# First two modulation chunks on TensorE in four column strips, in place of row sums on VectorE and GpSimd

## Chip, cores and metric

One core of a Trainium2 chip runs the kernel. The metric is the device time of one execution in microseconds; the time given for the kernel before is the median of three runs. TensorE multiplies matrices, VectorE, ScalarE and GpSimd work on tiles of up to 128 partitions, and transfers from device memory are issued by SyncE (its queue is SP's) and GpSimd.

## What is computed

One layer of a diffusion backbone in float32, for 512 latent tokens and 256 context tokens of 1024 channels. Only its beginning matters here: an RMS norm whose result is modulated by shift and scale, two of six chunks of `silu(c) @ w_mod + b_mod`, for the latent by `c` and for the context by `c_ctx`.

```python
def _modulate(x, g, shift, scale):
    return _rmsnorm(x, g) * (1.0 + scale) + shift

m_x = (silu(c) @ w_mod + b_mod).reshape(B, 6, 1, 1024)
m_c = (silu(c_ctx) @ w_mod + b_mod).reshape(6, 1024)
hc = _modulate(ctx, g_norm1, m_c[0], m_c[1])
pc = hc @ w_in[:, :1280]
hx = _modulate(x, g_norm1, m_x[:, 0], m_x[:, 1])
px = hx @ w_in
```

What follows takes `px` and `pc`: a recurrent branch (RG-LRU, five heads), a gMLP branch with spatial gating, their merge under two sigmoid gates, an output projection, a second norm, a channel mixer with a 3x3 convolution, and a final norm. Chunks 2 to 5 of the modulation are used there.

## The kernel before

Tokens lie along the free dimension and channels over the partitions ("channel-major"): 1024 channels are eight channel tiles of 128. Nearly every large product runs as three float32r matmuls: weights and activations are each split into two float32r parts that sum to the float32 value (`wh`, `wl`; `hxh`, `hxl`), and the low-by-low product is left out. The class `Weights` (line 55) loads weight blocks in the order in which TensorE takes them, through SP's queue into two buffers, casts the high part on ScalarE (line 95) and subtracts it on VectorE or GpSimd (line 97). `W.load` asks for a block's transfer, `W.prepare` splits up to a block, `W.take` hands over the next one.

The first stage (lines 218 to 355) is the one that the change touches.

- Loads, all on SP's queue: `crow` (both `c` vectors as 16 rows), `xc` (all 768 tokens, eight transfers of 384 KB), the packed parameters `sm`, then `w_mod` by channel tile (`wm`, 1 MB each, four buffers) alternating with the first weight blocks.
- Conditioning: `sig` is silu of `crow`; 16 matmuls against slices of the identity spread both vectors over all partitions (line 253), and copies bring them to `cbx` and `cbc`.
- Norm: squares on ScalarE (line 262), their sums over channel tiles on VectorE for the latent (line 263) and on GpSimd for the context (line 264), sums over partitions by a matmul with ones (line 274), root and reciprocal, and `spread_rows` (line 205) to bring the factor of every token to all partitions; the result is `rb`.
- Modulation of channel tile k: `mod_rows` takes the dot products of the rows of `wm` with `cbx` and `cbc`, four per tile (shift and scale, latent and context). The table `MOD_ON` says for each whether VectorE does it in one operation (line 303) or GpSimd multiplies (line 297) and ScalarE sums (line 298). `mod_cols` adds the bias and multiplies by `g1`. `mod_h` multiplies x by `rb` and scale (line 330, VectorE), casts the high part with the shift added (line 331, ScalarE) and makes the low part (line 332, VectorE).
- `products(k)` adds channel tile k's part to nine outputs that stay in PSUM (line 314): two tiles of `rx` for the latent, the same two for the context (`rxc`), two of `rg` and three of the merge's first gate `gr` (`NFIRST`). These are 27 matmuls for a tile, 21 of 512 columns and 6 (the context's) of 256; the other `gr` tiles are computed later, before the gates of heads that `GR_AT` names.

Two channel tiles are modulated ahead of the first products (`LEAD`), then one for each step. The build's scheduler decides the order of each engine's instructions: by the order in the program, except that one which it holds to be ready goes ahead of one that is not; `after` fixes an order by hand. On the chip each engine keeps the order it was given.

Chunks 2 to 5 of the modulation come later, row by row of `w_mod` from GpSimd's queue (lines 554 to 569), against `cbx` and `sc`. The change leaves them as they are; line 613, the spatial gating's float32 matmul, is also unchanged.

Of the kernel before, what the change touches and what calls it, by code (L numbers as in the profile page):

```python
# [42 lines left out]
# Columns of the packed per-channel parameters.  # L43
# [66 lines left out]
def hybrid_block(ctx: ExitStack, tc: tile.TileContext, a: dict, out: bass.AP):  # L110
# [107 lines left out]
    with pool("pro", side="right") as pro:  # L218
        crow = pro.tile([2 * KD, P], F32, name="crow")
        nc.sync.dma_start(crow, a["c_row"])  # L220
        xc = pro.tile([P, KD, TT], F32, name="xc")
        for k in range(KD):
            nc.sync.dma_start(xc[:, k, :], a["xc"][k])
        nc.sync.dma_start(sm, a["smalls"])
        wms = {}

        def load_mod(k):
            wms[k] = pro.tile([P, 2, D], F32, tag="wm", name=f"wm{k}", bufs=4)
            nc.sync.dma_start(wms[k], a["w_mod01"][k].rearrange("p (s c) -> p s c", s=2))
# [12 lines left out]
        # silu(c), silu(c_ctx) in every partition.  # L242
        sig = pro.tile([2 * KD, P], F32, name="sig")
        nc.scalar.activation(sig, crow, AF.Sigmoid)
        nc.vector.tensor_tensor(sig, sig, crow, op=ALU.mult)
        cb = (cbx, pro.tile([P, D], F32, name="cbc"))
        cbp = {}
        for n in range(2):
            for hf in range(2):
                pb = cbp[n, hf] = mm_tile(f"cb{n}{hf}")  # L250
                for q in range(4):
                    kk = KD * n + 4 * hf + q
                    nc.tensor.matmul(pb[:, q * P : (q + 1) * P], ident[: 2 * KD, kk : kk + 1].to_broadcast([2 * KD, P]), sig,
                                     start=True, stop=True)
        psc = mm_tile("psc")
        nc.tensor.transpose(psc[:, : 2 * KD], sig, ident[: 2 * KD, : 2 * KD])
        nc.vector.tensor_copy(sc, psc[:, :KD])
        sqs = pro.tile([P, TT], F32, name="sqs")
        nc.scalar.activation(sqs, xc[:, 0, :], AF.Square)
        for k in range(1, KD):  # L260
            sq = pro.tile([P, TT], F32, tag="sq", name=f"sq{k}", bufs=4)
            squared = nc.scalar.activation(sq, xc[:, k, :], AF.Square)
            nc.vector.tensor_tensor(sqs[:, TC:], sqs[:, TC:], sq[:, TC:], op=ALU.add)
            nc.gpsimd.tensor_tensor(sqs[:, :TC], sqs[:, :TC], sq[:, :TC], op=ALU.add)
        for (n, hf), pb in cbp.items():
            if (n, hf) != (1, 1):
                nc.vector.tensor_copy(cb[n][:, hf * T : (hf + 1) * T], pb)
        after(nc.scalar.copy(cb[1][:, T:], cbp[1, 1]), squared)
        # The latent's tokens first.
        rb = pro.tile([P, TT], F32, name="rb")  # L270
        for t0, n, slot in ((2, 4, 0), (0, 2, 1)):
            pss = aux_tile(f"pss{t0}", slot)
            for t in range(n):
                mm = nc.tensor.matmul(pss[:, t : t + 1], sqs[:, (t0 + t) * P : (t0 + t + 1) * P], ones[:, 0:1],
                                      start=True, stop=True)
                if t0 == 0 and t == 0:
                    after(mm, summed)
                summed = mm
            r = rstd_of(pro, pss[:, :n], f"n1{t0}", n)
            prb = aux_tile(f"rb{t0}", slot)[:, : n * P]  # L280
            spread_rows(prb, r, n)
            copied = nc.scalar.copy(rb[:, t0 * P : (t0 + n) * P], prb)
# [3 lines left out]
        gr_ps = {j: mm_tile(f"gr{j}") if j < 2 else aux_tile(f"gr{j}", 1) for j in range(NFIRST)}  # L286
# [4 lines left out]
        def mod_rows(k, n, ms):  # L291
            """Shift (2 n) and scale (2 n + 1) sums of channel tile k for x (n = 0) or ctx (n = 1)."""
            for s in range(2):
                o = ms[:, 2 * n + s : 2 * n + s + 1]
                if MOD_ON[k][2 * n + s] == "G":
                    junk = pro.tile([P, D], F32, tag="pjunk", name=f"pj{k}{s}{n}", bufs=3)
                    nc.gpsimd.tensor_tensor(junk, wms[k][:, s, :], cb[n], op=ALU.mult)  # L297
                    act = nc.scalar.activation(junk, junk, AF.Copy, accum_out=o)  # L298
                    if k == 0:
                        after(act, copied)  # L300
                else:
                    junk = pro.tile([P, D], F32, tag="junk", name=f"vj{k}{s}{n}", bufs=1)
                    nc.vector.scalar_tensor_tensor(junk, wms[k][:, s, :], 1.0, cb[n],  # L303
                                                   op0=ALU.mult, op1=ALU.mult, accum_out=o)

        def products(k, wh, wl):
            xs = ((hxh[:, k, :], hxl[:, k, :]), (hch[:, k, :], hcl[:, k, :]))
            outs = [(rx_ps[j][0], j, *xs[0]) for j in range(2)] + [(rx_ps[j][1], j, *xs[1]) for j in range(2)]
            outs += [(rg_ps[j], 2 + j, *xs[0]) for j in range(2)] + [(gr_ps[j], 4 + j, *xs[0]) for j in range(NFIRST)]
            for i, (o, j, xh, xl) in enumerate(outs):  # L310
                c = slice(j * P, (j + 1) * P)
                for n, (w, x) in enumerate(((wh, xh), (wh, xl), (wl, xh))):
                    first, last = k == 0 and n == 0, k == KD - 1 and n == 2
                    mm = nc.tensor.matmul(o, w[:, c], x, start=first and i != 3, stop=last and i != 2)
                    if (first or last) and i in (2, 3):
                        if i == 3:
# [5 lines left out]
        def mod_cols(k, ms, n0, n1):  # L322
            m = ms[:, 2 * n0 : 2 * n1].rearrange("p (n s) -> p n s", s=2)
# [608 lines left out]
```

## Time and profile before

| | |
|---|---|
| median of 3 runs | 1013.49 us (1010.37 to 1014.34) |
| profiled execution, span from first to last instruction | 1015.3 us |
| TensorE, matmuls busy | 956.4 us (94%) |
| VectorE busy | 710.9 us (70%) |
| ScalarE busy | 489.3 us (48%) |
| GpSimd busy | 150.1 us (15%) |

Of the profiled execution the profile gives the span and no other time, so the two stand side by side in the table. Busy time is an average over the whole kernel; what an engine is worth in one stage is read from the stretch in which the stage lies. "PE" is TensorE's matmuls, "PEld" its weight loads, "DVE" VectorE, "ACT" ScalarE, "POOL" GpSimd. Matmuls are pipelined, so that their listed durations overlap: what one costs in a row of them is the distance between starts.

### The profile page before, as it was taken

What the parts mean: (1) busy time and instruction counts of PE and PEld (TensorE: products, weight loads), DVE (VectorE), ACT (ScalarE), POOL (GpSimd) and SP (SyncE); (2) the same over time, 40 slices, a digit from 0 to 9 for tenths busy, and PEclk for the clock granted to TensorE, in tenths of its full rate; (3) what the DMA queues carried; (4) which work ended last, traced back from release to release, by engine and by line L of the source; (5) the groups of instructions that cost most, each with busy time, mean ns of one, the idle gap of its engine ahead of it and who ended that gap; (6) DMA issues with size and microseconds to landing.
All of it is one profiled execution on the core that took longest, in us unless ns stands there. A gap on an engine that the chain in (4) does not pass through costs nothing.

```text
span 1015.3 us, 11483 instructions
## 1 busy us (share of the span) xinstructions
PE 956.4 (94%) x4547; PEld 794.2 (78%) x4547; DVE 710.9 (70%) x894; ACT 489.3 (48%) x675; POOL 150.1 (15%) x113
## 2 busy tenths in 40 slices
PE   4568999999999999989999998999999999999997
PEld 4357888888888878878888888988767888887686
DVE  6999849696766776567653356598778437888864
ACT  5445697888799682114323334344333213333333
POOL 7661000000000011110100112212220003222020
PEclk9979999999999999999999999999999999999999
DMA  9422221222222247653632621122212332221232
GB/s 361 150 97 83 83 83 43 83 76 70 87 101 83 83 167 240 257 207 106 213 138 83 212 108 75 45 81 83 83 63 84 124 138 90 83 84 63 66 122 83
DMA packets 22325, 116.29 MB, mean 115 GB/s; under 512 B 2544, under 2 KB 2688, under 8 KB 13312
## 3 DMA queue, kind: packets, MB, share of 16 engines
q1 hardware_dynamic: 16448, 94.59, 25.8%
q0 software_dynamic: 5824, 20.97, 6.0%
q8 instruction: 35, 0.57, 0.2%
q14 instruction: 18, 0.15, 0.0%
HBM read 113.46 MB, written 2.10 MB: 114 GB/s over the span
## 4 chain that ended last, share of the span: by engine, by line
PE 59%; DVE 21%; ACT 9%; issue 6%; DMA 3%; POOL 1%; SPq 0%; ACTq 0%; POOLq 0%; DVEq 0%
DVE acc L798 8%; PE d L142 4%; PE d L141 4%; PE d L143 4%; PE up L143 4%; PE up L141 4%; PE up L142 4%; DVE wl L97 3%; DMA wmod<-in_w_mod 2%; ACT wh L95 2%; PE pg L142 1%; PE pg L141 1%; PE pg L143 1%; DVE vj L303 1%; PE gg L143 1%
## 5 line engine op out<-in xcount | busy, mean ns | idle before, releaser
L95 ACT CAST wh<-raw 128x1024 fp32r<-128x1024 f32 (+1 forms) x155 | 161.2, 1043 | 225.1 <-PE d L143 44.1
L97 DVE TENSOR_TENSOR wl<-raw,wh 128x1024 fp32r<-128x1024 f32 (+1 forms) x131 | 159.2, 1217 | 114.1 <-ACT wh L95 113.5
L798 DVE SCALAR_TENSOR_TENSOR acc<-gpad,sm,acc 128x512 f32<-128x512 f32 x176 | 159.4, 916 | 21.4 <-ACT acc L795 17.3
L143 PE MATMUL up<-h2h,wl 128*128 128x512 f32 (+1 forms) x384 | 145.2, 378 | 6.8 <-POOL wl L97 6.8
L141 PE MATMUL up<-h2h,wh 128*128 128x512 f32 (+1 forms) x384 | 144.7, 377 | 1.4 <-ACT wh L95 1.4
L142 PE MATMUL up<-h2l,wh 128*128 128x512 f32 (+1 forms) x384 | 143.8, 375 | 0.0
L97 POOL TENSOR_TENSOR wl<-raw,wh 128x1024 fp32r<-128x1024 f32 x24 | 61.8, 2575 | 291.7 <-ACT wh L95 279.7
L143 PEld LDWEIGHTS up<-h2h,wl 128*128 128x128 f32 x384 | 73.1, 190 | 23.2 <-POOL wl L97 8.8
L141 PEld LDWEIGHTS up<-h2h,wh 128*128 128x128 f32 x384 | 73.2, 191 | 14.8 <-ACT wh L95 2.8
L142 PEld LDWEIGHTS up<-h2l,wh 128*128 128x128 f32 x384 | 73.1, 190 | 12.5
L801 ACT ACTIVATE acc<-acc 128x512 f32<-128x512 f32 x22 | 13.9, 632 | 134.4 <-DVE acc L798 134.4
L142 PE MATMUL d<-wl,fh 128*128 128x512 f32 (+1 forms) x186 | 72.1, 388 | 0.1
L141 PE MATMUL d<-wh,fh 128*128 128x512 f32 (+1 forms) x186 | 71.1, 382 | 0.0
L143 PE MATMUL d<-wh,fl 128*128 128x512 f32 (+1 forms) x186 | 70.8, 381 | 0.0
L556 POOL DMA_DIRECT2D wmod<-in_w_mod x32 | 16.9, 528 | 244.7 <-DVE yrl L539 123.2
L559 DVE SCALAR_TENSOR_TENSOR wmod<-wmod,cbx 128x1024 f32<-128x1024 f32 x24 | 29.3, 1222 | 29.8 <-DMA wmod<-in_w_mod 29.7
L142 PEld LDWEIGHTS d<-wl,fh 128*128 128x128 f32 x186 | 35.0, 188 | 8.4 <-DVE wl L97 1.4
L141 PEld LDWEIGHTS d<-wh,fh 128*128 128x128 f32 x186 | 34.9, 188 | 8.1
L143 PEld LDWEIGHTS d<-wh,fl 128*128 128x128 f32 x186 | 34.9, 188 | 7.3
L297 POOL TENSOR_TENSOR pj<-wm,cbc 128x1024 f32<-128x1024 f32 x13 | 37.5, 2909 | 9.8 <-ACT pj L298 9.2
L142 PE MATMUL pr<-yrl,wh 128*128 128x512 f32 x80 | 31.7, 396 | 0.0
L143 PE MATMUL pr<-yrh,wl 128*128 128x512 f32 x80 | 31.7, 396 | 0.0
(318 smaller groups left out, 2271.9 us busy)
## 6 DMA issues: line engine op xcount, KB each, us to landing
raw<-in_w_up SPq DMA_DIRECT2D x22, 1024.0 KB, 4.8
wmod<-in_w_mod POOLq DMA_DIRECT2D x32, 512.0 KB, 4.3
raw<-in_w_down SPq DMA_DIRECT2D x22, 512.0 KB, 3.3
wm<-in_w_mod SPq DMA_DIRECT2D x8, 1024.0 KB, 8.6
raw<-in_w_lru SPq DMA_DIRECT2D x5, 1024.0 KB, 4.7
raw<-in_w_pr SPq DMA_DIRECT2D x5, 1024.0 KB, 6.9
raw<-in_w_rx SPq DMA_DIRECT2D x4, 1024.0 KB, 4.8
raw<-in_w_rg SPq DMA_DIRECT2D x4, 1024.0 KB, 4.8
```

The lines of the kernel that those rows point to most:

```text
L95: nc.scalar.copy(h[:, :n], r)
L97: eng.tensor_tensor(l[:, :n], r, h[:, :n].bitcast(F32), op=ALU.subtract)
L141: nc.tensor.matmul(o, wh, xh, start=first, stop=False)
L142: nc.tensor.matmul(o, wh, xl, start=False, stop=False)
L143: nc.tensor.matmul(o, wl, xh, start=False, stop=last)
L297: nc.gpsimd.tensor_tensor(junk, wms[k][:, s, :], cb[n], op=ALU.mult)
L303: nc.vector.scalar_tensor_tensor(junk, wms[k][:, s, :], 1.0, cb[n], op0=ALU.mult, op1=ALU.mult, accum_out=o)
L556: nc.gpsimd.dma_start(wm, a["w_mod25"][n - 2, k])
L559: nc.vector.scalar_tensor_tensor(wm, wm, 1.0, cbx, op0=ALU.mult, op1=ALU.mult, accum_out=m)
L798: nc.vector.scalar_tensor_tensor(acc, pad[:, dy : dy + ROWS, dx : dx + GRID_W], col("ffw", 9 * i + q), acc, op0=ALU.mult, op1=ALU.add)
L801: nc.scalar.activation(accf, accf, AF.Gelu_apprx_tanh)
```

## The change

The sums of the first two modulation chunks go to TensorE. `w_mod` is laid out so that a tile `wm` holds, for shift and scale, eight blocks with 128 rows of `w_mod` over the partitions and the 128 channels of the tile along the columns. `c32` holds silu of both `c` vectors in columns 0 and 1 of 32, the others zero; it is the stationary operand of 32 float32 matmuls for a channel tile. Each writes 32 partitions of PSUM: four strips of the array's columns, one for each of shift and scale and each half of the eight blocks. ScalarE copies the 128 x 128 result, and one more matmul with `sel` adds the two halves and turns the rows into four columns. No row sums are left on VectorE and GpSimd.

The latent's tokens are loaded and normed ahead of the context's, which become a transfer of their own (`ctx`, 1 MB) behind three tiles of `w_mod`; the context's sum of squares moves from GpSimd to VectorE; `w_mod`'s first tile is loaded ahead of x. In the products the context's outputs come last. `NFIRST` becomes 2, so the first weight blocks have 768 columns in place of 896, and one `gr` tile more is computed later. `cbx` is now made after the first stage, from a load of `c` over all partitions on GpSimd's queue. The residual's later load of x takes the whole rows of the new `xc`.

```diff
-NFIRST = 3
-GR_AT = {4: (3, 4), 5: (5, 6, 7)}
-MOD_ON = ("VVGG", "VVGG", "VVGG", "VGGG", "VVGV", "GVGG", "VGVG", "GVGV")
+NFIRST = 2
+GR_AT = {4: (2, 3), 5: (4, 5, 6, 7)}
...
         nc.sync.dma_start(crow, a["c_row"])
+        wms = {}
+
+        def load_mod(k):
+            wms[k] = pro.tile([P, 2, KD, P], F32, tag="wm", name=f"wm{k}", bufs=4)
+            nc.sync.dma_start(wms[k].rearrange("p s k c -> p (s k c)"), a["w_mod01"][k])
+
+        load_mod(0)
         xc = pro.tile([P, KD, TT], F32, name="xc")
         for k in range(KD):
-            nc.sync.dma_start(xc[:, k, :], a["xc"][k])
+            nc.sync.dma_start(xc[:, k, TC:], a["xc"][k])
         nc.sync.dma_start(sm, a["smalls"])
-        load_mod(0)
         load_mod(1)
         W.load(0)
         load_mod(2)
+        nc.sync.dma_start(xc[:, :, :TC], a["ctx"].rearrange("p (k t) -> p k t", k=KD))
         W.load(1)
         load_mod(3)
...
+        sig = pro.tile([2 * KD, P], F32, name="sig")
+        nc.scalar.activation(sig, crow, AF.Sigmoid)
+        nc.vector.tensor_tensor(sig, sig, crow, op=ALU.mult)
+        c32 = pro.tile([P, KD, 32], F32, name="c32")
+        nc.gpsimd.memset(c32, 0.0)
+        psc = mm_tile("psc")
+        nc.tensor.transpose(psc[:, : 2 * KD], sig, ident[: 2 * KD, : 2 * KD])
+        nc.vector.tensor_copy(c32[:, :, 0:2], psc[:, : 2 * KD].rearrange("p (n k) -> p k n", n=2))
+        nc.vector.tensor_copy(sc, psc[:, :KD])
+
+        sel = pro.tile([P, 2, 2], F32, name="sel")
+        quarters = ident.rearrange("p (s h c) -> p s h c", s=2, h=2)
+        nc.gpsimd.tensor_tensor(sel, quarters[:, :, 0, 0:2], quarters[:, :, 1, 0:2], op=ALU.add)
...
+        mss = {}
+
+        def mod_cols(k):
+            pm = aux_tile(f"pm{k}", 1)
+            for kk in range(KD // 2):
+                for s in range(2):
+                    for h in range(2):
+                        at = 64 * s + 32 * h
+                        nc.tensor.matmul(pm[at : at + 32, :P], c32[:, 4 * h + kk, :], wms[k][:, s, 4 * h + kk, :],
+                                         start=kk == 0, stop=kk == KD // 2 - 1, tile_position=(0, at))
+            rows = pro.tile([P, P], F32, tag="mrow", name=f"mrow{k}", bufs=2)
+            nc.scalar.copy(rows, pm[:, :P])
+            nc.tensor.matmul(pm[:, P : P + 4], rows, sel.rearrange("p s n -> p (s n)"), start=True, stop=True)
+            ms = mss[k] = pro.tile([P, 2, 2], F32, tag="ms", name=f"ms{k}", bufs=4)
+            nc.vector.tensor_tensor(ms, pm[:, P : P + 4].rearrange("p (s n) -> p n s", s=2),
+                                    bm1[:, k].unsqueeze(1).to_broadcast([P, 2, 2]), op=ALU.add)
+            nc.vector.tensor_scalar(ms[:, :, 1], ms[:, :, 1], col("g1", k), None, op0=ALU.mult)
...
+        def norm_of(lo, hi):
+            sq = lambda k: pro.tile([P, T], F32, tag="sq", name=f"sq{lo}{k}", bufs=4)[:, : hi - lo]
+            nc.scalar.activation(sqs[:, lo:hi], xc[:, 0, lo:hi], AF.Square)
+            for k in range(1, KD):
+                q = sq(k)
+                nc.scalar.activation(q, xc[:, k, lo:hi], AF.Square)
+                nc.vector.tensor_tensor(sqs[:, lo:hi], sqs[:, lo:hi], q, op=ALU.add)
+            n = (hi - lo) // P
+            pss = aux_tile(f"pss{lo}", 0)
+            for t in range(n):
+                nc.tensor.matmul(pss[:, t : t + 1], sqs[:, lo + t * P : lo + (t + 1) * P], ones[:, 0:1],
+                                 start=True, stop=True)
+            r = rstd_of(pro, pss[:, :n], f"n1{lo}", n)
+            prb = aux_tile(f"rb{lo}", 0)[:, : hi - lo]
             spread_rows(prb, r, n)
+            return nc.scalar.copy(rb[:, lo:hi], prb)
+
+        mod_cols(0)
+        norm_of(TC, TT)
+        mod_cols(1)
+        normed = norm_of(0, TC)
...
         def products(k, wh, wl):
             xs = ((hxh[:, k, :], hxl[:, k, :]), (hch[:, k, :], hcl[:, k, :]))
-            outs = [(rx_ps[j][0], j, *xs[0]) for j in range(2)] + [(rx_ps[j][1], j, *xs[1]) for j in range(2)]
-            outs += [(rg_ps[j], 2 + j, *xs[0]) for j in range(2)] + [(gr_ps[j], 4 + j, *xs[0]) for j in range(NFIRST)]
+            outs = [(rx_ps[j][0], j, *xs[0]) for j in range(2)] + [(rg_ps[j], 2 + j, *xs[0]) for j in range(2)]
+            outs += [(gr_ps[j], 4 + j, *xs[0]) for j in range(NFIRST)] + [(rx_ps[j][1], j, *xs[1]) for j in range(2)]
...
-        W.prepare(LEAD - 1)
-        for k in range(LEAD):
-            mod_tile(k)
+        W.prepare(0)
+        mod_h(0, 0)
+        mod_h(0, 1)
+        W.prepare(1)
+        mod_h(1, 0)
+        mod_h(1, 1)
         for k in range(KD):
             if k + 4 < KD:
                 load_mod(k + 4)
-            blk = W.take(ahead=1)
             if k in (0, 2):
                 W.load(k // 2 + 2)
+            blk = W.take(ahead=1)
             if k + LEAD < KD:
-                mod_tile(k + LEAD)
+                mod_cols(k + LEAD)
+                mod_h(k + LEAD, 0)
+                mod_h(k + LEAD, 1)
             products(k, *blk)
 
     W.boost = 1000
+
+    nc.gpsimd.dma_start(cbx, a["c_b"])
+    with pool("cb") as cp:
+        cs = cp.tile([P, D], F32, name="cs")
+        after(nc.scalar.activation(cs, cbx, AF.Sigmoid), normed)
+        nc.vector.tensor_tensor(cbx, cbx, cs, op=ALU.mult)
```

Left out are comments, the removed functions `mod_rows` and `mod_tile` and the removed norm, whose lines stand in the kernel above, the layout of the inputs, and in `products` the two conditions that name the context's outputs by their place.

## Rows read from the trace of the kernel before

**Rows 1.** The page's first line.

```profile
span 1015.3 us, 11483 instructions
```

**Rows 2.** By stretch: us, busy us of PE, PEld, DVE, ACT, POOL; PEclk, DMA share, GB/s.

```profile
0.00:28.60 28.60, 12.68 (x57) 12.20 (x57) 18.65 (x26) 16.25 (x25) 21.58 (x20) 1.00 0.92 364
28.60:82.50 53.90, 33.96 (x115) 24.93 (x115) 53.90 (x56) 22.81 (x40) 34.73 (x13) 0.89 0.25 93
82.50:103.90 21.40, 21.38 (x102) 18.27 (x103) 19.43 (x45) 13.84 (x23) 0.26 (x6) 0.97 0.32 108
103.90:1015.00 911.10, 888.37 (x4275) 738.84 (x4273) 618.88 (x771) 436.36 (x590) 93.48 (x75) 0.99 0.31 108
```

**Rows 3.** Waits of TensorE, 0 to 104 us: total, times, longest (us).

```profile
PE rx L314 <- DVE hxl L332: 14.1, 3, 6.1
PE rx L314 <- ACT wh L95: 7.7, 1, 7.7
```

**Rows 4.** Chain of waits, 72 to 106 us: start, us, what.

```profile
79.93 2.55 DVE hcl L332
...
98.40 1.36 PE rx L314 x6
99.76 0.71 PE rxc L314 x6
100.47 1.39 PE rg L314 x6
101.86 2.04 PE gr L314 x9
```

**Rows 5.** VectorE's groups, 0 to 104 us: busy us, mean ns.

```profile
L303 DVE SCALAR_TENSOR_TENSOR vj<-wm,cbx 128x1024 f32<-128x1024 f32 x12 | 18.8, 1564 | 0.0
...
L303 DVE SCALAR_TENSOR_TENSOR vj<-wm,cbc 128x1024 f32<-128x1024 f32 x3 | 3.6, 1212 | 0.0
```

**Rows 6.** VectorE's lines 332 and 97, to 104 us: ns min/median/max.

```profile
L332 DVE SCALAR_TENSOR_TENSOR hxl<-xc,ms,hxh x8: 735/742/2861, 31.5 to 95.9; 128x512 fp32r<-128x512 f32 x8
L332 DVE SCALAR_TENSOR_TENSOR hcl<-xc,ms,hch x8: 471/476/2611, 37.7 to 96.6; 128x256 fp32r<-128x256 f32 x8
...
L97 DVE TENSOR_TENSOR wl<-raw,wh x10: 1076/1081/1218, 35.7 to 100.6; 128x896 fp32r<-128x896 f32 x8, 128x1024 fp32r<-128x1024 f32 x2
```

**Rows 7.** GpSimd's products, 0 to 110 us: busy us, mean ns.

```profile
L297 POOL TENSOR_TENSOR pj<-wm,cbc 128x1024 f32<-128x1024 f32 x13 | 37.5, 2909 | 9.8 <-ACT pj L298 9.2 <-DVE sqs L263 0.6
```

**Rows 8.** Line 613 (ns min/median/max) and TensorE's timeline around it.

```profile
L613 PEld LDWEIGHTS s<-wst,vg x64: 187/192/192, 432.9 to 483.8; 128*128 128x128 f32 x64
L613 PE MATMUL s<-wst,vg x64: 270/275/275, 433.1 to 483.9; 128*128 128x128 f32 x64
...
433.15 1.05 PE L613 MATMUL s<-wst,vg 128*128 128x128 f32 x8
433.96 0.47 PE L141 MATMUL u<-hxh,wh 128*128 128x512 f32 x1
```

**Rows 9.** Timeline, 12 to 21 us: start us, us, instruction.

```profile
12.45 0.84 ACT L262 ACTIVATE sq<-xc 128x768 f32<-128x768 f32 x1 [0.17 <-DMA xc<-in_xc]
...
14.27 1.18 DVE L263 TENSOR_TENSOR sqs<-sqs,sq 128x512 f32<-128x512 f32 x1
...
15.51 2.72 PE L274 MATMUL pss<-ones,sqs 128*128 128x1 f32 x12 [5.19 <-DVE sqs L263]
...
18.09 2.06 PE L205 MATMUL rb<-ident,n12r 128*128 128x128 f32 x8
...
20.18 0.58 ACT L282 COPY rb<-rb 128x512 f32<-128x512 f32 x1 [1.65 <-PE rb L205]
```

**Rows 10.** DMA rate, 0 to 27.5 us in 40 slices of 0.69 us.

```profile
GB/s 0 0 12 161 340 291 384 322 268 308 349 380 411 398 420 405 425 468 441 417 405 429 441 423 396 417 429 422 439 405 407 425 427 413 426 417 441 417 429 393
```

**Rows 11.** ScalarE's timeline: a square of 256 columns.

```profile
611.78 0.42 ACT L679 ACTIVATE osq<-x1c 128x256 f32<-128x256 f32 x1 [2.43 <-DVE x1c L674]
```

More of the change, by code (lines that the diff above doesn't have):

```diff
@@ L220, in hybrid_block @@
         nc.sync.dma_start(crow, a["c_row"])
+        wms = {}
[3 more added lines that the diff above has]
+        load_mod(0)
         xc = pro.tile([P, KD, TT], F32, name="xc")
         for k in range(KD):
-            nc.sync.dma_start(xc[:, k, :], a["xc"][k])
+            nc.sync.dma_start(xc[:, k, TC:], a["xc"][k])
         nc.sync.dma_start(sm, a["smalls"])
[L225 to L229, printed above, removed]
-        load_mod(0)
         load_mod(1)
@@ L241, in hybrid_block @@
         nc.vector.tensor_scalar(bm1[:, :, 1], col("bmod", KD, KD), 1.0, None, op0=ALU.add)
[L243 to L254, printed above, removed]
@@ L255, in hybrid_block @@
-        psc = mm_tile("psc")
-        nc.tensor.transpose(psc[:, : 2 * KD], sig, ident[: 2 * KD, : 2 * KD])
-        nc.vector.tensor_copy(sc, psc[:, :KD])
-        sqs = pro.tile([P, TT], F32, name="sqs")
[L259 to L268, printed above, removed]
-        rb = pro.tile([P, TT], F32, name="rb")
-        for t0, n, slot in ((2, 4, 0), (0, 2, 1)):
-            pss = aux_tile(f"pss{t0}", slot)
-            for t in range(n):
[L274 to L280, printed above, removed]
-            spread_rows(prb, r, n)
-            copied = nc.scalar.copy(rb[:, t0 * P : (t0 + n) * P], prb)
+        mss = {}
@@ L285, in hybrid_block @@
+        mod_cols(0)
+        norm_of(TC, TT)
+        mod_cols(1)
+        normed = norm_of(0, TC)
         rxc = aux_tile("rxc", 0)
-        gr_ps = {j: mm_tile(f"gr{j}") if j < 2 else aux_tile(f"gr{j}", 1) for j in range(NFIRST)}
+        gr_ps = {j: mm_tile(f"gr{j}") for j in range(NFIRST)}
         for j in range(2):
@@ L289, in hybrid_block @@
             rg_ps[j] = mm_tile(f"rg{j}")
[L291 to L304, printed above, removed]
         def products(k, wh, wl):
             xs = ((hxh[:, k, :], hxl[:, k, :]), (hch[:, k, :], hcl[:, k, :]))
-            outs = [(rx_ps[j][0], j, *xs[0]) for j in range(2)] + [(rx_ps[j][1], j, *xs[1]) for j in range(2)]
-            outs += [(rg_ps[j], 2 + j, *xs[0]) for j in range(2)] + [(gr_ps[j], 4 + j, *xs[0]) for j in range(NFIRST)]
+            outs = [(rx_ps[j][0], j, *xs[0]) for j in range(2)] + [(rg_ps[j], 2 + j, *xs[0]) for j in range(2)]
+            outs += [(gr_ps[j], 4 + j, *xs[0]) for j in range(NFIRST)] + [(rx_ps[j][1], j, *xs[1]) for j in range(2)]
+            c0 = 4 + NFIRST
             for i, (o, j, xh, xl) in enumerate(outs):
@@ L313, in products @@
                     first, last = k == 0 and n == 0, k == KD - 1 and n == 2
-                    mm = nc.tensor.matmul(o, w[:, c], x, start=first and i != 3, stop=last and i != 2)
-                    if (first or last) and i in (2, 3):
-                        if i == 3:
+                    mm = nc.tensor.matmul(o, w[:, c], x, start=first and i != c0 + 1, stop=last and i != c0)
+                    if (first or last) and i >= c0:
+                        if i > c0:
                             after(mm, shared)
@@ L320, in hybrid_block, with mod_h @@
         PARTS = ((TC, TT, hxh, hxl), (0, TC, hch, hcl))
[L322 to L327 removed]
+        def mod_h(k, n):
             lo, hi, dh, dl = PARTS[n]
[L329 to L330 removed]
+            x, sh = xc[:, k, lo:hi], mss[k][:, n, 0:1]
+            nc.vector.scalar_tensor_tensor(x, x, mss[k][:, n, 1:2], rb[:, lo:hi], op0=ALU.mult, op1=ALU.mult)
             nc.scalar.activation(dh[:, k, :], x, AF.Identity, bias=sh)
             nc.vector.scalar_tensor_tensor(dl[:, k, :], x, sh, dh[:, k, :].bitcast(F32), op0=ALU.add, op1=ALU.subtract)
[L334 to L346 removed]
+        W.prepare(0)
[4 more added lines that the diff above has]
+        mod_h(1, 1)
         for k in range(KD):
@@ L379, in hybrid_block @@
         nc.vector.scalar_tensor_tensor(z, lam, -1.0, lam, op0=ALU.mult, op1=ALU.max)
-        nc.scalar.activation(z, z, AF.Exp, scale=-1.0)
+        after(nc.scalar.activation(z, z, AF.Exp, scale=-1.0), normed)
         nc.vector.tensor_scalar(s, z, 2.0, None, op0=ALU.add)
@@ L650, in hybrid_block @@
     for k in range(KD):
-        nc.gpsimd.dma_start(x1c[:, k, :], a["xc"][k][:, TC:])
+        nc.gpsimd.dma_start(x1c[:, k, :], a["xc"][k])
     x1 = x1p.tile([P, 4, D], F32, name="x1")
@@ L864, in _layout @@
     o = {}
-    o["xc"] = f(np.concatenate([v["ctx"][0], v["x"][0]], axis=0).T.reshape(KD, P, TT))
+    o["ctx"] = f(np.asarray(v["ctx"][0]).T.reshape(KD, P, TC).transpose(1, 0, 2).reshape(P, KD * TC))
+    o["c_b"] = f(np.broadcast_to(np.asarray(v["c"][0])[None, :], (P, D)))
+    o["xc"] = f(np.asarray(v["x"][0]).T.reshape(KD, P, T))
     convw = np.asarray(v["conv_w"][0]).reshape(4, NR, P).transpose(2, 1, 0).reshape(P, 40)
```

15 lines of the change are left out of this document (1 added, 14 removed).

## Prediction

> **What bounds the kernel now.** The table of busy time by stretch comes first [rows 2]. From 103.9 us to the end TensorE is busy 888.37 of 911.10 us: that part costs what its matmuls cost. The loss is at the front. From 28.6 to 82.5 us VectorE is busy all 53.90 us and TensorE only 33.96, so TensorE stands idle for 20 us. The waits of TensorE name the cause [rows 3]: 14.1 us for `hxl`, the last thing VectorE makes of a channel tile, and 7.7 us for the first weight cast, which is queued on ScalarE behind the sums. The chain of waits says the same [rows 4]: VectorE ends `hcl` at 82.5 us, and from there the products run back to back, the last `gr` group ending at 101.86 + 2.04 = 103.9 us. So the bound is VectorE's work per channel tile up to 82.5 us, and then TensorE.
>
> Why VectorE is slow shows in two views. Its row sums are 12 x 1.564 + 3 x 1.212 = 22.4 us [rows 5]. And its other passes stretch: the split `hxl` takes 0.74 us in its median and 2.86 at worst, `hcl` 0.48 and 2.61 [rows 6]; the long ones lie in the stretch in which GpSimd multiplies, 2.9 us a piece [rows 7]. After the change GpSimd has no such work.
>
> **Form of the sum.** All that follows 103.9 us is the same work, except that the third gate tile leaves the first products and comes back as one of the later ones, where TensorE is the bound. In the products it costs 2.04 / 3 x 8 = 5.45 us [rows 4], and as much later. So the change is worth E + 5.45 - 103.9, with E the new end of the products. One tile's products become rx 1.36 + rg 1.39 + two thirds of gr 1.36 + rxc 0.71 = 4.82 us [rows 4].
>
> **What is removed.** 15 row sums of VectorE, 17 products of GpSimd with their sums on ScalarE, the copies of `cbx` and `cbc`, and the 16 broadcast matmuls. What is left to VectorE for a tile is two passes and two splits (2 x (0.74 + 0.48)), a weight split of 1.08 x 768/896 = 0.93 and two tiny operations: some 3.7 us [rows 6], under TensorE's 4.82 for the products alone. VectorE drops off the path, and TensorE, now with the sums as well, is next.
>
> **What is added on TensorE, M for each tile.** The strips are 32 float32 matmuls, 128 rows deep, 32 columns wide, 128 columns streamed. Before has no such form. The nearest is the full-width float32 matmul of the spatial gating, also 128 columns streamed [rows 8]: the 32 in the code appear as 64 pairs of load and matmul, and eight pairs take 433.96 - 433.15 = 0.81 us, 0.101 a pair; the load alone lasts 0.192, the matmul 0.275, and they overlap. Bounds: if four strips run at once, 64 x 0.101 / 4 = 1.6 us; if one after another, 64 x 0.101 = 6.5 us; if each load (a quarter of 0.192, as 32 of 128 columns) comes into the open too, 64 x (0.101 + 0.048) = 9.5 us. I take the middle: the two pairs of one matmul use the same strip, so the second must wait for the first, while the next strip's first pair can run beside it. That is 32 x 0.101 = 3.2 us. For the selector matmul behind it (two pairs), the wait for ScalarE's copy, and going into strips and back, I add 0.5 us a tile.
>
> The Trainium skill, TensorEngine Tiling (Array Packing), Theoretical Speedup and Key Properties, has tiles work independently, loads and matmuls in parallel, with up to four times the rate at 32 columns. By it M would be 1.6 us, the first bound; no strip is in this trace.
>
> **Start of the loop.** The bytes ahead of the latent's last tile stay 3.1 MB (w_mod tile 0 goes ahead, the context's thirds go out), so x is there at 12.4 us, when the last square starts now [rows 9]. That square and an add end near 12.45 + 0.84 + 0.7 = 14; from there to the copied `rb` is 20.76 - 15.45 = 5.3 us now [rows 9], so 19.3. With a pass of 0.74 and a cast taken for as long the latent's products start at 21. The context lands later: 4.1 MB more at 420 GB/s [rows 10] is 22.3 us. Eight squares of 0.42 [rows 11] and an add bring 26.1; its part of the norm, 5.3 less two tiles' matmuls, 3.4; pass and cast 1.0; rxc 0.71: the first tile's products end at 31.3 us. In front of that lie w_mod tiles 0 to 2, of which the first has TensorE to itself from about 5.7 us (1.06 MB through by 5.5 [rows 10]). Early matmuls are slower: eight pairs of the same shape take 2.06 us at 18 us and 0.81 at 433 [rows 8, 9], a ratio as of 1.2 to 2.4 GHz, though the profile prints a granted clock of 1.00 there. I let that be covered by the wait for the context.
>
> **The sum.** E = 31.3 + 7 x 4.82 + 5 x (3.2 + 0.5) = 83.5; 83.5 + 5.45 - 103.9 = -14.9 us. The profiled execution's span is 1015.3 us [rows 1], 1.8 above the median of 1013.5, so I take the difference over to the median: 998.6 us.
>
> **Moved and small.** SP's queue: the context's load stands behind three w_mod tiles and one weight block, and is priced above. The fourth weight block's load is now asked for ahead of the split that frees its buffer; SP waits there, and w_mod tile 7 queues behind it. It is needed only ahead of the sixth products, some 15 us later, and costs nothing unless SP is held longer than that. GpSimd's queue gets the 512 KB load of `c_b`; no other work stands there now. Sigmoid and product of `cbx` are two passes of some 1.2 us [rows 5], hidden in ScalarE's idle time (22.81 busy of 53.90 [rows 2]) and VectorE's; first used at the merge. Without cover they cost 2.4 us, and a table load. One PSUM bank holds the strips' sums, so the next tile's strips wait for VectorE's add; the products between them cover it.
>
> **Rivals.**
> *Four strips at once.* M = 1.6, with the sum above: 31.3 + 33.7 + 5 x 2.1 + 5.45 - 103.9 = -22.9, 990.6 us. For it: 32 columns use a quarter of the array. Against: in this trace pairs start strictly one behind another.
> *No overlap: the strips don't do what they are meant to.* They run singly, or issue binds. Then TensorE is the bound from the landing of w_mod tile 0: 5.7 + 8 x (6.5 + 0.5) + 38.6 (eight products) + 5.8 (the norm's matmuls, 2.72 + 1.5 x 2.06 [rows 9]) = 106.1; + 5.45 - 103.9 = +7.7, 1021 us. For it: 0.101 a pair is the fastest that the trace shows.
> *Slower: the weight loads in the open.* M = 9.5: 5.7 + 8 x 10 + 38.6 + 5.8 = 130.1; +31.7, 1045 us. Place: between the strips' matmuls. It decides from M = 5.5 on, where the same sum comes to no change. Against: loads hide behind matmuls in every full-width row here [rows 8].
> The Trainium skill, TensorE: Matmul & The Clock Gate, Part 3, says that loads overlap matmuls in flight only when the row group differs, and all four strips have the same one; by that this rival holds. The full-width rows, of one row group too, overlap all the same, so I give it little.
> *The context's norm goes first on VectorE or ScalarE* and the latent's products wait for it: they cost 18 x 0.23 = 4.1 us [rows 4] behind it, and some stalls with them: 5 us of the gain, about 1004 us.
>
> **How the numbers follow.** Middle overlap 0.42, four at once 0.26, none 0.15, loads in the open 0.09, context first 0.08. 0.5% is 5.1 us, about what a measurement of this kernel can tell. Faster by more than that needs M under 4.9: 0.71. Within it, parts of the third, first and last cases: 0.10. Slower: 0.19. The range runs from four strips at once with a little more room, 988, to the case without overlap, 1022 with its rounding; beyond are the loads in the open and a better start, some 0.15.
>
> **What would show it.** Right: products ending near 84 us, VectorE idle in the stretch, `hxl` at 0.74 in every instance, strips of a tile in 3.2 us, TensorE hardly waiting after 31 us. Wrong: a strip block of over 5.5 us; TensorE waiting for `rows` or for `hch` in each tile; products starting after 25 us; or a later stage, past the products, in which TensorE waits more than its 23 us of now.

## Result and profile after

The median falls from 1013.91 us (1010.37 to 1016.05, four runs) to 990.18 us (989.27 to 990.89, four runs): a ratio of 0.976, 95% interval 0.9739 to 0.9781, or 22.2 to 26.5 us less. The forecast of 998.6 us had the sign and the form of the sum right and was 8.4 us too long. The time that came is the 990.6 us of the rival with four strips at once, in part by luck, as the section after the experiments shows.

The page's first line, to be held against [rows 1]:

```profile
span 988.1 us, 11916 instructions
```

The busy time by stretch, as in [rows 2] (stretch, its length, then busy us of PE, PEld, DVE, ACT and POOL, PEclk, DMA share, GB/s). The stretches are cut where the products begin and end:

```profile
0.00:24.70 24.70, 8.97 (x86) 7.34 (x86) 7.47 (x20) 10.38 (x18) 1.93 (x11) 1.00 0.94 355
24.70:75.50 50.80, 50.36 (x404) 39.67 (x405) 34.30 (x79) 27.07 (x50) 0.25 (x6) 1.00 0.47 180
75.50:988.10 912.60, 892.32 (x4300) 742.42 (x4298) 623.44 (x769) 440.59 (x595) 92.77 (x75) 0.99 0.31 108
```

The middle row is the change. In the stretch where TensorE was busy 33.96 of 53.90 us before, it is now busy 50.36 of 50.80; VectorE, which was never idle there, is busy 34.30. The bound has passed from VectorE to TensorE.

The waits of TensorE from the start to 76 us, as in [rows 3] (total, times, longest):

```profile
PE pm L265 <- DVE c L245: 7.2, 1, 7.2
...
PE rb L203 <- DVE n1256r L197: 1.9, 1, 1.9
...
PE rx L317 <- ACT wh L93: 1.0, 1, 1.0
```

The 14.1 us for `hxl` are gone and the 7.7 us for the first weight cast have become 1.0. The largest that is left, 7.2 us for the copy of `c`, lies ahead of the first strips. No matmul waits for `hxl` any more; the weight loads wait for it once, 0.5 us.

VectorE's line 330, as line 332 in [rows 6] (ns min/median/max, first to last start):

```profile
L330 DVE SCALAR_TENSOR_TENSOR hxl<-xc,ms,hxh x8: 744/747/752, 24.9 to 63.6; 128x512 fp32r<-128x512 f32 x8
L330 DVE SCALAR_TENSOR_TENSOR hcl<-xc,ms,hch x8: 475/478/483, 42.6 to 64.3; 128x256 fp32r<-128x256 f32 x8
```

No instance is long any more; before, the longest took 2.861 and 2.611 us.

The chain of waits, as in [rows 4] (start, us, what):

```profile
17.18 1.28 ACT L196
...
19.01 2.08 PE rb L203 x8
21.09 1.91 PE pm L265 x32
...
27.59 1.01 PE pm L265 x32
...
43.19 1.50 PE rxc L317 x11
44.69 1.01 PE pm L265 x32
45.70 0.91 PE rxc L317 x6
...
59.71 1.01 PE pm L265 x32
...
66.03 1.39 PE rx L317 x6
...
70.85 1.39 PE rx L317 x6
72.24 1.36 PE rg L317 x6
73.60 1.36 PE gr L317 x6
74.96 0.71 PE rxc L317 x6
75.67 0.23 PE rx L139
```

One tile's strips are 32 pairs of load and matmul, from 16 matmuls in the code, and take 1.01 us; early, ahead of the products, the same block takes 1.91. From 59.71 to 66.03 us one step with a tile's sums takes 6.32 us; from 66.03 to 70.85 one without takes 4.82. So the sums of a tile cost some 1.5 us in all, with the selector and with going into strips and back. The first tile's context outputs come from 42.2 us on, and the products end at 75.67, against 103.9 before.

What follows is the same work but for the third gate tile. Two stretches of each kernel, before (first two lines) and after, in the columns of the table above:

```profile
103.90:428.00 324.10, 322.73 (x1611) 271.94 (x1610) 233.51 (x275) 236.03 (x303) 11.23 (x21) 1.00 0.31 112
428.00:484.00 56.00, 52.52 (x257) 43.99 (x256) 38.01 (x70) 17.92 (x24) 3.17 (x6) 0.97 0.45 162
```

```profile
75.50:405.00 329.50, 328.12 (x1635) 276.52 (x1634) 235.73 (x273) 240.41 (x309) 11.06 (x21) 1.00 0.32 112
405.00:457.00 52.00, 50.95 (x256) 42.90 (x255) 37.90 (x70) 17.57 (x24) 3.17 (x6) 1.00 0.45 161
```

Up to the spatial gating it takes 329.5 - 324.1 = 5.4 us longer, with 24 matmuls more: the third gate tile, priced at 5.45. So the account is 75.5 - 103.7 (the start of the head's first matmul in each) + 5.4 = -22.8 us, against -23.7 by the medians. The two spans differ by more, 27.2 us: the gating stretch is 4.0 us shorter in this pair. In it TensorE waits 3.5 us for `wl` before and 1.1 after, and its matmuls are busy 1.6 us less, at a granted clock of 1.00 in place of 0.97. In the profiles of the experiments that wait lies anywhere from 0 to 3.1 us, whatever the kernel, so the difference isn't counted as an effect.

### The profile page after: what moved, and what is told of

Same layout as the page of the kernel before. It is cut to its first block, busy times and chain, and to the rows that moved or that the text cites. A ratio compares the mean times of both kernels' runs of the same rounds, so it can differ in the third digit from the quotient of the medians.

```text
span 988.1 us, 11916 instructions
## 1 busy us (share of the span) xinstructions
PE 951.6 (96%) x4787; PEld 789.4 (80%) x4787; DVE 665.2 (67%) x867; ACT 478.0 (48%) x661; POOL 95.0 (10%) x92
## 4 chain that ended last, share of the span: by engine, by line
PE 65%; DVE 16%; ACT 8%; issue 6%; DMA 3%; POOL 1%; SPq 0%; ACTq 0%; DVEq 0%; POOLq 0%
DVE acc L797 8%; PE d L140 4%; PE d L141 4%; PE d L139 4%; PE up L139 4%; PE up L141 4%; PE up L140 4%; DVE wl L95 2%; DMA wmod<-in_w_mod 2%; ACT wh L93 2%; PE pg L139 2%; PE pg L140 2%; PE pg L141 2%; PE gg L141 1%; PE gg L140 1%
## 5 line engine op out<-in xcount | busy, mean ns | idle before, releaser
L140 PEld LDWEIGHTS up<-h2l,wh 128*128 128x128 f32 x384 | 73.3, 191 | 12.5
L474 DVE TENSOR_TENSOR i<-i,xr 128x768 f32<-128x768 f32 x20 | 18.9, 954 | 19.7 <-ACT i L467 19.7
```

The lines of the kernel that those rows point to most:

```text
L140: nc.tensor.matmul(o, wh, xl, start=False, stop=False)
L474: nc.vector.tensor_tensor(i[u], i[u], xr[h][:, u % 2, :], op=ALU.mult)
```

## Experiments

"End" is the start of the head's first `rx` matmul in a profile, where the products have just ended: 103.7 us before, 75.5 us in the changed kernel. Ratios are to the kernel before on the same chip. All kernels compute the whole layer.

### Four matmuls of one strip in a row

The theory: a tile's strips are cheap because neighbours work on different strips. Only the order of the 16 matmuls changes.

```diff
-            for kk in range(KD // 2):
-                for s in range(2):
-                    for h in range(2):
+            for s in range(2):
+                for h in range(2):
+                    for kk in range(KD // 2):
```

> The changed kernel with the loops of a tile's sixteen strip matmuls turned round: the four of one strip come one behind another. Theory (neighbours in TensorE's queue on different strips run side by side, neighbours on one strip don't): a tile's 32 pairs go from 1.01 us to 32 x 0.101 = 3.2 us. Six tiles in the dense stretch give 6 x 2.2 = 13 us, the second tile, at the lower clock ahead of the first products, another 4 to 5: about 1008 us. Rival (a pair of 32 columns is short by itself, 0.03 us, whatever stands beside it): 1.0 us a tile as before, 990 us.

Measured: 1002.93 us beside 1015.09, ratio 0.9901 [0.9875, 0.9927]; end at 87.9 us. Its chain of waits, one tile:

```profile
70.07 0.71 PE rxc L317 x6
70.78 2.39 PE pm L265 x32
73.17 0.67 PE rx L317 x2
```

The same 32 pairs take 2.39 to 2.49 us in place of 1.01, 0.075 to 0.078 a pair against 0.032. So the order is worth most of the strips' speed. It is under the 3.2 us of the expectation: a pair starts every 0.075 us although a load alone is listed with 0.106 at least, so pairs in one strip still overlap in part. Of the 12.4 us by which the end is later, 3.9 lie ahead of the products, which start at 28.6 us and not at 24.7 (the two early blocks take 4.51 and 3.87 us), and 6 x 1.4 = 8.4 in the six tiles behind.

### No strips: w_mod stationary, two columns streamed

The blocks of `w_mod` are loaded as weights, 128 wide, and the two vectors are streamed; no copy and no selector.

```diff
-                        nc.tensor.matmul(pm[at : at + 32, :P], c32[:, 4 * h + kk, :], wms[k][:, s, 4 * h + kk, :],
...
-            nc.scalar.copy(rows, pm[:, :P])
-            nc.tensor.matmul(pm[:, P : P + 4], rows, sel.rearrange("p s n -> p (s n)"), start=True, stop=True)
+            for s in range(2):
+                for kk in range(KD):
+                    nc.tensor.matmul(pm[:, P + 2 * s : P + 2 * s + 2], wms[k][:, s, kk, :], c32[:, kk, 0:2],
+                                     start=kk == 0, stop=kk == KD - 1)
```

> The changed kernel without strips: w_mod's 128 x 128 blocks as the stationary operand, two columns of silu streamed, sixteen full-width matmuls a tile, and neither copy nor selector, since the sums come out by channel. Theory (strips side by side are what makes the sums cheap): each of 32 pairs costs what a full-width load costs, 0.101 us, 3.2 us a tile; 6 x (3.2 - 1.0 - 0.3) = 11 us in the dense stretch and 4 ahead of it: about 1005 us. Rival (it is enough that TensorE sums; the copy and the selector eat what the strips save): 990 to 993 us.

Measured: 1025.64 us beside 1015.09, ratio 1.0116 [1.0085, 1.0147]; end at 112.1 us. It is 1.2% slower than the kernel before, and neither theory said so. By stretch (columns as above):

```profile
43.00:49.70 6.70, 6.70 (x35) 5.67 (x34) 3.02 (x7) 1.85 (x5) 0.00 (x0) 1.00 0.12 50
49.80:53.60 3.80, 3.80 (x33) 3.80 (x32) 1.28 (x3) 3.61 (x6) 0.00 (x0) 0.91 0.00 0
53.60:58.00 4.40, 4.40 (x11) 3.46 (x12) 4.14 (x9) 2.63 (x4) 0.00 (x0) 0.50 0.02 4
58.20:65.00 6.80, 6.80 (x35) 6.80 (x33) 0.57 (x2) 0.00 (x0) 0.00 (x0) 0.50 0.00 0
```

TensorE has no gap here, yet its granted clock falls from 1.00 (2.4 GHz) to 0.50 (1.2 GHz) with a block of 32 pairs that stream two columns each. The block at 49.8 us costs 3.8 us, at a granted 0.91, the one at 58.2 us 6.6 at 0.50, and the products behind it run at half too: in its chain six `gr` matmuls take 1.36 us at 45.8 us and 2.56 at 55.7. Over 31.5 to 112.1 us the mean granted clock is 0.77. Is the loss the clock, or the full-width loads?

### The same loads with 128 columns streamed

The roles are as in the change, silu stationary and `w_mod` streamed, but silu is padded to 128 columns, so that each matmul fills the array's width.

```diff
-        c32 = pro.tile([P, KD, 32], F32, name="c32")
+        c32 = pro.tile([P, KD, P], F32, name="c32")
...
+            for s in range(2):
+                for kk in range(KD):
+                    nc.tensor.matmul(pm[:, s * P : (s + 1) * P], c32[:, kk, :], wms[k][:, s, kk, :],
+                                     start=kk == 0, stop=kk == KD - 1)
```

> The changed kernel without strips, the other way round from the two-column form: silu's two columns padded to 128 are the stationary operand, w_mod's blocks are streamed, 128 columns each, sixteen full-width matmuls a tile; a 256-column copy and two selectors. The array takes as long as in the two-column form, 32 pairs of 0.101 to 0.12 us. Theory (in the two-column form the clock fell to its lower level because the blocks stream two columns, and that cost more than the loads): here the clock stays up, the tile costs 3.2 + 0.5 us, the products end near 90 to 95 us (75.7 in the changed kernel, 112 in the two-column form): about 1006 to 1010 us. Rival (long full-width float32 loads bring the clock down, whatever is streamed): products end past 105 us, 1020 us or more.

Measured: 1003.26 us beside 1017.72, ratio 0.9876 [0.9844, 0.9908]; end at 88.0 us, a little earlier than the 90 to 95 expected. From its chain of waits the early norm and two blocks, and the stretch of the products:

```profile
18.34 1.16 PE rb L203 x8
19.50 3.57 PE pm L263 x32
...
42.69 3.57 PE pm L263 x32
46.26 0.70 PE rx L317 x3
...
22.80:88.20 65.40, 65.40 (x424) 58.11 (x423) 35.75 (x81) 28.42 (x51) 0.25 (x6) 1.00 0.40 153
```

At the full width 32 pairs take 3.57 us, 0.112 a pair, and the clock stays at 1.00. A two-column block takes about as long while the clock is up (3.8 above), so the 112.1 - 88.0 = 24.1 us between the two forms go with the clock and not with the loads. From the first product to the end it is 80.6 us there and 65.2 here, 15.4 us, with the mean clock of 0.77 that the page shows. The other 8.7 lie ahead of it (the products start at 31.57 us there, at 22.82 here): the two early blocks take 6.98 and 6.63 us there against 5.39 and 3.57 here, in the second a ratio as of the two levels, though the page prints 1.00 for both. The two forms differ in two things, the columns streamed (2 and 128) and the operand held in the array (`w_mod`, or silu with 126 columns of zeros); no run here separates them.

The strips gain 88.0 - 75.5 = 12.5 us over the full width. From the first product to the end they gain 65.2 - 50.8 = 14.4, and they lose 1.9 ahead of it. Behind its long first block (5.39 us, from 10.26) the full-width kernel spreads the norm's factors in 1.16 us, at 18.34; the changed kernel, whose first block takes 1.94 us, needs 2.08 for the same eight pairs, at 19.01. So early in the changed kernel TensorE works at about half the rate, with a printed clock of 1.00, where the full-width kernel had the full rate already.

### The kernel before without GpSimd's products

All row sums on VectorE: 17 more for it, none for GpSimd.

```diff
-MOD_ON = ("VVGG", "VVGG", "VVGG", "VGGG", "VVGV", "GVGG", "VGVG", "GVGV")
+MOD_ON = ("VVVV",) * 8
```

> The kernel before with all 32 row sums on VectorE, none on GpSimd. Theory (GpSimd's products stretch VectorE's passes, so that taking work to GpSimd cost VectorE more than it saved): hxl 0.74 us in all eight instances; VectorE has 32 x 1.285 = 41 us of sums and 8 x (2 x (0.74 + 0.48) + 1.08 + 0.4) = 31 us of the rest from 15.4 us on, ends the last hcl near 89 us (97 before), and the products end near 96: about 1006 us. Rival (the number of row sums on VectorE is the bound; GpSimd's share was a relief): 17 x 1.285 = 22 us more on VectorE, about 1025 to 1035 us.

Measured: 1000.24 us beside 1015.09, ratio 0.9881 [0.9835, 0.9926]; end at 90.7 us, where 96 was expected. One line of the kernel before gives over half of what the whole change gives. VectorE's groups (busy us, mean ns), first of the kernel before to 104 us:

```profile
L330 DVE SCALAR_TENSOR_TENSOR xc<-xc,ms,rb 128x512 f32<-128x512 f32 (+1 forms) x16 | 19.4, 1246 | 0.2
...
L332 DVE SCALAR_TENSOR_TENSOR hxl<-xc,ms,hxh 128x512 fp32r<-128x512 f32 x8 | 12.2, 1526 | 0.0
...
L324 DVE TENSOR_TENSOR ms<-ms,bm 128x4 f32<-128x4 f32 (+1 forms) x10 | 5.6, 571 | 0.0
```

The same groups with all sums on VectorE, to 91 us:

```profile
L303 DVE SCALAR_TENSOR_TENSOR vj<-wm,cbx 128x1024 f32<-128x1024 f32 x16 | 19.4, 1214 | 0.0
...
L330 DVE SCALAR_TENSOR_TENSOR xc<-xc,ms,rb 128x512 f32<-128x512 f32 (+1 forms) x16 | 9.3, 611 | 0.0
L332 DVE SCALAR_TENSOR_TENSOR hxl<-xc,ms,hxh 128x512 fp32r<-128x512 f32 x8 | 6.0, 745 | 0.0
...
L324 DVE TENSOR_TENSOR ms<-ms,bm 128x4 f32<-128x4 f32 (+1 forms) x10 | 1.5, 153 | 0.0
```

The passes, `hxl` and the bias add fall by 10.1, 6.2 and 4.1 us; `hcl` (10.2 to 3.8) and line 325 (4.2 to 2.2) by 8.4 more; the row sum itself falls from 1.564 us [rows 5] to 1.214, some 4 us over the 15 that were VectorE's. So GpSimd took 17 x 1.29 = 22 us of sums off VectorE (1.21 and its readout of 0.08) and cost it some 33 us in longer passes. The same line also takes GpSimd's sums off ScalarE (17.7 us, and 3.2 of readouts); TensorE's wait for the first weight cast falls from 7.7 to 3.8 us. So the 13.0 us at the end of the products are not shown to be GpSimd's alone; the next experiment leaves ScalarE's work as it is.

### GpSimd's load put back into the changed kernel

Two products of 128 x 1024 for each tile, whose results are not used, on GpSimd.

```diff
+        def pool_load(k):
+            for s in range(2):
+                junk = pro.tile([P, D], F32, tag="pjunk", name=f"pj{k}{s}", bufs=3)
+                src = wms[k][:, s].rearrange("p k c -> p (k c)")
+                nc.gpsimd.tensor_tensor(junk, src, src, op=ALU.mult)
```

> The changed kernel with GpSimd given two products of 128 x 1024 for each channel tile again, about as many as before (16 for 17), whose results nobody uses; nothing else. Theory (a VectorE pass that meets a GpSimd product waits some 2 us for it, as hxl's 2.86 us for 0.74 in the kernel before): hxl and hcl stretch again, VectorE's 3.9 us a tile grow past the 5.9 that TensorE needs, and the products end 10 to 20 us later: 1000 to 1010 us. Rival (VectorE has room now, and GpSimd's products cost nothing): 990 to 992 us.

Measured: 1002.11 us beside 1017.72, ratio 0.9859 [0.9831, 0.9888]; end at 88.7 us, 13.2 later. Line 330 and the stretch of the products:

```profile
L330 DVE SCALAR_TENSOR_TENSOR hxl<-xc,ms,hxh x8: 742/751/2379, 25.4 to 77.0; 128x512 fp32r<-128x512 f32 x8
...
25.00:88.70 63.70, 55.01 (x405) 42.84 (x405) 46.96 (x80) 27.08 (x50) 21.22 (x16) 0.89 0.37 141
```

From its chain of waits, and TensorE's largest wait from 20 to 90 us:

```profile
31.03 0.17 DVE ms L271
...
32.16 2.35 DVE xc L328
...
36.80 2.04 DVE sqs L285
...
PE rx L317 <- ACT wh L93: 8.3, 2, 7.6
```

`hxl` reaches 2.379 us again, and four of the context's adds take 1.94 to 2.04 us each where they took 0.44, all in the chain of waits. ScalarE's squares wait 5.3 us for those adds to free their buffers, and the next weight block's cast stands behind the squares: that is TensorE's wait of 7.6 us, up to 44.12. VectorE comes to the low part only behind the adds: in the chain it ends at 46.87 us and the next `rx` starts at 46.91. TensorE is idle 8.7 us of the stretch, 0.4 without the load; its matmuls are busy 55.01 us in place of 50.36, at a granted clock of 0.89. No wait of TensorE for a transfer appears, though GpSimd also holds the `wm` buffers longer. GpSimd's work hands the path no data, and still lengthens it.

The Trainium skill, SBUF — State Buffer, Who interferes with whom, states that a VectorE operation with two inputs in SBUF and a GpSimd operation that reads SBUF exclude each other, and that the one issued second waits for the whole of the first. This case agrees: `hxl` takes 0.74 us alone, up to 2.38 beside GpSimd's products of 1.88 to 2.61 us; the add of line 271, one of whose inputs is in PSUM, took 0.17 us at 31.03, amid four products that ran from 27.77 to 36.25.

### The kernel before with two gate tiles first

```diff
-NFIRST = 3
-GR_AT = {4: (3, 4), 5: (5, 6, 7)}
+NFIRST = 2
+GR_AT = {4: (2, 3), 5: (4, 5, 6, 7)}
```

> The kernel before with two gate tiles in the first products, not three, and nothing else. Theory (this part is a cost by itself, paid to free a PSUM bank): VectorE's bound up to 82.5 us stays, less a shorter weight split (8 x 0.15 us); four tiles behind it save 4 x 0.68 = 2.7 us; the gate tile costs 5.45 us later: 1 to 2 us slower, about 1015 us. Rival (part of the gain comes from it): 5 us faster or more.

Measured: 1017.5 us beside 1015.09, ratio 1.0037 [1.0014, 1.0059]; end at 102.4 us. The rival is excluded. Where VectorE is the bound, 5.45 us less of matmuls bring the end forward by only 1.3 us, and the tile is paid for later. This part of the change is a price by itself: it frees the PSUM bank of the strips' sums.

### The context first

```diff
         xc = pro.tile([P, KD, TT], F32, name="xc")
+        nc.sync.dma_start(xc[:, :, :TC], a["ctx"].rearrange("p (k t) -> p k t", k=KD))
...
-        nc.sync.dma_start(xc[:, :, :TC], a["ctx"].rearrange("p (k t) -> p k t", k=KD))
...
         mod_cols(0)
+        normed = norm_of(0, TC)
         norm_of(TC, TT)
         mod_cols(1)
-        normed = norm_of(0, TC)
```

> The changed kernel with the context loaded and normed ahead of the latent, nothing else. Theory (once the products start, TensorE has no gap, so the end follows the start one for one): the load puts the latent back by 1 MB at 0.42 MB/us, 2.5 us, and the context's eight squares of 0.42 and seven adds stand ahead of its own, up to 3 more: 993 to 996 us. Rival (the start is not on the path, since the context's products wait for their norm either way): 990 us.

Measured: 992.28 us beside 1017.72, ratio 0.9756 [0.9719, 0.9793]; end at 78.5 us. As the time did not tell it from the changed kernel, it ran once more, beside that kernel on one chip, in five rounds each:

> The kernel with the context loaded and normed first. Its products ended 3.0 us later than the changed kernel's. Theory (one for one): 3 us, 0.3%, slower than the changed kernel on the same chip. Rival: the same.

> The changed kernel itself, once more, beside the two of which a single chip's runs must tell 3 us apart. Ratio to the kernel before 0.976 as measured, products ending at 75.5 us.

Measured: 991.89 us, ratio 0.9764 [0.9738, 0.979], end at 76.7 us, against the changed kernel's 991.08 us, 0.9757 [0.9732, 0.9782], 75.2 us. The profiles put the end 1.5 to 3.0 us later, the times 0.8 us with intervals that overlap almost wholly: inconclusive. The latent's place ahead of the context is worth a few us at most; it isn't where the gain is.

### An earlier start

The chain of the changed kernel has 1.28 us of table load and the second tile's strips and copy (21.09 to 23.30) ahead of the first products, and the copy of `c` waits on VectorE behind the first add of squares. This kernel loads the table for the root at the start, puts the first adds behind the copy of `c`, casts the first weights ahead of the copy of `rb`, and takes the second tile's sums after the first tile's high part.

```diff
+        warm = nc.scalar.activation(pro.tile([P, 1], F32, name="warm"), ones[:, 0:1], AF.Sqrt)
+        after(warm, nc.scalar.activation(sig, crow, AF.Sigmoid))
...
-                nc.vector.tensor_tensor(sqs[:, lo:hi], sqs[:, lo:hi], q, op=ALU.add)
+                after(nc.vector.tensor_tensor(sqs[:, lo:hi], sqs[:, lo:hi], q, op=ALU.add), early)
...
         mod_cols(0)
+        W.prepare(0)
         norm_of(TC, TT)
+        first = mod_h(0, 0)
         mod_cols(1)
```

Here `early` is VectorE's copy of `c` into `sc`. Left out are the orders that hold the squares behind the table, the copy of `rb` behind the first cast, and the second tile's copy and the second cast behind `first`.

> The changed kernel with three things moved in its first 25 us, all arithmetic the same: ScalarE's table for the square root is loaded at the start and not between the latent's sums and their root (1.28 us on the chain there); the first weight block's high part is cast while ScalarE waits for the norm and not behind the first activation cast (0.8 us); the second channel tile's copy goes behind that cast (0.6 us). Theory (the end follows the start of the products one for one): the products start near 22 us and not at 24.7, 987.5 us, 2.7 us faster than the changed kernel. Rival (the context's part, or the weights, set the end): 990 us.

Measured: 987.97 us beside 1017.72, ratio 0.9715 [0.9687, 0.9742]; end at 72.5 us. Again on the chip of the repeated kernel above:

> The kernel with the square-root table, the first weight cast and the second tile's copy moved in the first 25 us. Its products ended 3.0 us earlier than the changed kernel's. Theory (everything behind them is one for one): 3 us, 0.3%, faster than the changed kernel on the same chip. Rival (the rest takes it up): the same.

Measured: 987.35 us beside that kernel's 991.08, ratio 0.9717 [0.9692, 0.9743] against 0.9757; end at 72.7 us against 75.2. The first 25 us on that chip, of the changed kernel and of this one:

```profile
0.00:25.00 25.00, 9.49 (x87) 7.79 (x88) 7.99 (x21) 11.00 (x18) 1.93 (x11) 1.00 0.94 357
```

```profile
0.00:25.00 25.00, 11.80 (x105) 9.50 (x109) 10.46 (x23) 11.77 (x20) 1.93 (x11) 1.00 0.94 357
```

TensorE has done 2.3 us more by then. It is the fastest version, by 3.7 us in the medians on one chip, though the intervals of the two ratios still touch. With TensorE full from the first product to the last, what the start gains comes out at the end.

## Why the prediction was right, and where it was off

- **The bound and the form of the sum: right.** E + 5.45 - 103.9 holds: the later stretch measured +5.4 us, and with E = 75.5 the sum gives -22.95, inside the measured 22.2 to 26.5.
- **VectorE off the path: right.** No matmul waits for `hxl`, VectorE is busy 34.30 us of 50.80, and `hxl` is at its short time throughout. That GpSimd's products were part of the cause is shown by putting them back into the changed kernel, which costs 13.2 us at the end of the products. Taking them out of the kernel before gives 13.0 us; that the two agree so closely is chance, since that run also adds row sums to VectorE and takes sums off ScalarE.
- **M, the strips of a tile: the term that failed.** The prediction and the section on the change count 32 strip matmuls for a tile, and the prediction doubles them to 64 pairs. The doubling is right (the gating's 32 in the code do appear as 64 pairs); the count isn't. The loops are 4 x 2 x 2, so there are 16 matmuls, seen as 32 pairs. The overlap was off as well: "the middle", two pairs of one strip one after another, would be 16 x 0.101 = 1.6 us with the right count, and the runs show 1.01, 0.0316 a pair, a factor of 3.2 against 0.101 and of 3.5 against the 0.112 of the full width in the same place. With all that hangs on it a tile's sums cost 1.5 us, not 3.2 + 0.5. The argument for the middle, that neighbours in one strip must wait, was sound in kind: in the turned order a tile's strips take 2.4 us.
- **By the Trainium skill, TensorEngine Tiling (Array Packing), Theoretical Speedup**, four times was the limit; 3.2 to 3.5 is what these runs show. Of the Trainium skill's rule in TensorE: Matmul & The Clock Gate, Part 3, that loads overlap only with another row group, this case shows the opposite: the strips' loads last 0.106 us at least, and a pair starts every 0.032 us though all strips share a row group. The rival built on it did not come.
- **The start of the products: 24.7 us, not 21.** The adds of the latent's squares end at 15.19 us, 1.2 later than taken. Not in the sum were the table load (1.28 us), the second tile's copy ahead of the first activation cast (0.7) and the first weight cast behind it (0.8). The earlier-start kernel took back 2.5 to 3.0 us of this. The early slowness of TensorE, which the prediction saw and let be covered by the wait for the context, stood open in part, as that wait was not on the path.
- **The path through the first tile's end at 31.3 us: wrong.** The sum has TensorE wait for the context up to there. The context's matmuls come only from 42.2 us on, three tiles' worth of them up to 46.61. The context's norm was late: behind the copy of its `rb` (38.66) a table load of 1.28 us and the sigmoid for `cbx` of 1.06 stand on ScalarE ahead of `hch`. The order of the instructions put the other tiles' latent products into the gap, and TensorE stayed full. So the end is its start plus its work: 24.7 + 8 x 4.82 + 6 x 1.5 + 1.1 (the context's norm on TensorE) = 73.4 us; the other 2 are waits of 0.4 us and slower matmuls right behind the start. The forecast's form with M as measured, 31.3 + 33.7 + 5 x 1.5, gives 72.5, 3 us too early.
- **The small items: right.** SP's queue held nothing up, the load of `c_b` is in no wait, `cbx`'s product is 1.23 us on a VectorE with room. The sigmoid's table load did stand ahead of the context's passes, as above.
- **The signs.** Of those for being right, VectorE's idle time, `hxl` and a TensorE that hardly waits after 31 us came; the end near 84 us and 3.2 us for a tile's strips did not. Of those for being wrong none was met: the start at 24.7 us came near the 25 that was named, and matmuls waited for `rows` three times, 1.2 us in all. After the products TensorE is idle 912.60 - 892.32 = 20.3 us, against 22.7 before.

That the time fell on a rival's value by so little (990.6 against 990.2) is luck in part. Its overlap did come, at 3.2 to 3.5 of four; but its 1.6 + 0.5 us a tile, from the doubled count, was 0.6 too long, 3 us over five tiles, and the rest of its sum was 3 us too short. So its end of the products is 75.5 us too.

## What to carry to other kernels

Before work is shared out to GpSimd, price what it does to VectorE's own passes in the same stretch: here 22 us were taken off and 33 us put on. Skinny float32 matmuls belong into column strips with neighbours on different strips; behind blocks that stream two columns only, look at the granted clock. Once TensorE is full from the first product on, look for the rest of the gain ahead of that product.

## What was not expected of the hardware

- A run of float32 matmuls that stream two columns brought TensorE's granted clock from 1.00 to 0.50 with no gap in its records, and the products behind ran at half speed; streaming 128 columns in the same number of pairs, with the operands' roles exchanged, it stayed at 1.00. Against the strips it turned a loss of 12.5 us into one of 36.6.
- Column strips of float32 reach 0.0316 us a pair with strips alternating, 0.075 to 0.078 within a strip, 0.112 at the full width.
- Beside GpSimd's products even VectorE's 128 x 4 adds took 0.57 us in the mean, against 0.15 without.
- The early strips took 1.91 us against 1.01 later, a ratio as of the clock's two levels, while the page gives that stretch a granted clock of 1.00. The same eight pairs of the norm took 2.08 us there and 1.16 in the full-width kernel, behind a longer first block. The two-column kernel, behind a block of 6.98 us, still took 2.07. A printed 1.00 this early doesn't tell the rate, and what brings it up stays open. Whether other work ahead of the norm would make the changed kernel faster was not run.
